# Two halves of the probabilities' lower parts on POOL, and transposes 30 matmuls behind their tile

## The chip, the cores and the metric

The kernel runs on one core of a Trainium2 chip. The metric is the device time of one execution in microseconds. Engines are named as in the profile: PE (TensorE, with PEld for its weight loads), DVE (VectorE), ACT (ScalarE), POOL (GpSimd), SP (SyncE, which issues the DMAs here).

## What is computed

A two-layer diffusion backbone over 1024 latent tokens and 256 context tokens with 1024 channels. Layer 0 mixes tokens with a convolution module, layer 1 with grouped-query attention (16 query heads, 4 key heads, head width 64); each layer ends in a squared-ReLU MLP with 4096 hidden channels. The part that matters here, from the reference:

```python
def gqa_project(h, w_qkv, q_norm, k_norm):
    qkv = h @ w_qkv
    q = qkv[..., :nq]...   # 16 heads of 64
    k = qkv[..., nq:nq + nk]...   # 4 heads of 64
    v = qkv[..., nq + nk:]...
    return rms_norm(q, q_norm), rms_norm(k, k_norm), v

ql = apply_axial_rope(ql, tables)
kl = apply_axial_rope(kl, tables)
...
s = jnp.einsum('bkgqd,bkld->bkgql', q, k).astype(jnp.float32) * (q.shape[-1] ** -0.5)
p = jax.nn.softmax(s, axis=-1).astype(v.dtype)
return jnp.einsum('bkgql,bkld->bkgqd', p, v)
...
def sq_relu_mlp(h, w1, w2):
    return jnp.square(jax.nn.relu(h @ w1)) @ w2
```

## The kernel before

Every matmul of a product works on float32 data split in two parts: a high part (rounded to float32r, made by ACT or DVE) and a lower part (the difference, made by POOL or DVE). A product is three matmuls, high by high, low by high and high by low (`mm3`, L213 to 219).

*Weights.* `unit` (L191 to 211) loads 128x1024 of weights into a `raw` buffer, ACT makes the high part, POOL the lower part in two instructions of 512 columns (or DVE in one of 1024). Both parts lie in a tile `wsp` of the ring `w8` with 5 buffers. While `self.six` names spare tiles, every sixth unit goes to these instead, and is then called `wx`.

*Layer 0's MLP and the projection.* The MLP runs over three token blocks of 416 to 432 columns, each in 8 chunks `c` of 4 hidden tiles: matmuls `ps<-h` (w1), then `ps<-hb` (w2). In the last block, `hook` interleaves layer 1's projection at the ends of chunks. The tokens are taken as A (0 to 384, three tiles of 128), D (384 to 512 and 1024 to 1280, three tiles) and C (512 to 1024, four tiles). `qkv_mm` (L924 to 956) makes for group g = 0 (keys and values), 1 and 2 (queries, 8 heads each) the product of each tile in a PSUM tile `pa`; after a tile's last matmul `qkv_post` (L958 to 989) follows:

- `head_norm`: ACT squares, DVE sums by head (`vh`, L872), takes the reciprocal root in small steps (`rs_s`, `rs_y`, L233 to 236) and multiplies (`kn`, L876).
- `head_parts`: `kn` times the cosines into `o` (POOL, L892), `kn` with halves swapped times the sines (`t`, DVE, L896), their sum (L898); then ACT makes the high part of `qs` or `ks` (L899) and DVE the lower (L900).
- `transpose_out` (L903 to 912): for each four heads four PE transposes into a PSUM tile `tp`, ACT's copy into the single buffer `sb`, and SP's store to `qt` or `kt` in DRAM.

A and D pass `late` empty, C passes it set. The code calls `transpose_out` directly behind `head_parts`. A scheduler orders each engine's instructions by dependencies and priorities, so that some matmuls of the next tile can stand between a tile's last matmul and its transposes. The engines run what they have strictly in their order.

*Attention.* Eight groups `n` (two blocks of 512 queries, four key heads), each with 40 steps `u`, one for each of 4 query heads and 10 key tiles. A step's `stage1` (L1074 to 1089): two matmuls make the scores `sT` (L1077, L1078), ACT the exponentials `e` (L1080), then the high part `p[:, 0]` (DVE's cast at L1083 in odd steps, ACT at L1085 in even ones) and the lower part `p[:, 1]` at L1087: by DVE in every fourth step, in every second at a group's ends and in the last group, else by POOL. `stage2`, five steps later, is three matmuls into `O` (L1093 to 1095). Beside the steps, PE makes the scores of the next group once more for their row maxima (L1040), which DVE reduces out of two PSUM banks (`m`, L1042), and at the end of a group DVE and POOL make the output's parts (`of`, `at`, `atl`).

Last comes layer 1's MLP (after 2186 us), which the change does not touch.

Of the kernel before, what the change touches and what calls it, by code (L numbers as in the profile page):

```python
# [103 lines left out]


LAG = 5
PT = ['rawm', 'sc', 'qs', 'raw', 'raw', 'raw']
MX0, MXS = 4, 38
HM, HS = 2, [1]
LM, LN, L0, L1 = 4, 2, 2, 38  # L110
WL = [0, 1, 2, 3, 4, 5, 6, 7]
PRE = [15, 30]
BUFS = {"w8": 5, "raw": 3, "rawm": 1, "xu": 3, "hl": 2, "hb": 1, "tmp": 5, "acc": 3, "sc": 1, "qs": 1, "ks": 1,
# [14 lines left out]
class Kern:  # L128
# [84 lines left out]
    def mm3(self, ps, pairs, first=True, last=True):  # L213

        n = len(pairs)
        for i, ((wh, wl), (ah, al)) in enumerate(pairs):
            for t in range(3):
                self.nc.tensor.matmul(ps, lhsT=(wh, wl, wh)[t], rhs=(ah, ah, al)[t], start=first and i == t == 0,  # L218
                                      stop=last and i == n - 1 and t == 2)

    def kpairs(self, w, a, N):
        return [((w[0](k), w[1](k)), (a[0](k)[:, :N], a[1](k)[:, :N])) for k in range(KT)]
# [404 lines left out]
    def layer0(self):  # L627
# [42 lines left out]
        def hook(b, c):  # L670
            if b < 2 and c == HCC[0]:
                self.drain(conv[b + 1])
                self.pw2(b + 1)
                n2[b] = self.norm2_block(b + 1, pl=N2P[b], dve_lo=ND[N2D[b]])
                self.bg.insert(0, n2[b])
            if b == 0 and c == 7:
                self.six = (("qs",), ("rawm",))
                self.bg.append(self.modq)
            if b == 2 and c == 1:
                self.drain(self.modq)  # L680
                self.six = (("sc",), ("rawm",))
            if b < 2 and c == 7:
                self.drain(n2[b])
            if b == 2 and c == 0:
                nc.sync.dma_start(out=self.X2[:, :, 0:80], in_=self.xs[1][:, :, 96:176])
            if b == 2 and c == HCC[1]:
                self.need((1, "cctx", 0))
                self.qkv_setup()
                n2["A"] = self.qkv_norm("A", [(0, 384)], pl=AP[0], dve_lo=ND[AD[0]])
                self.bg.insert(0, n2["A"])  # L690
            if b == 2 and c == HCC[2]:
                self.drain(n2["A"])
                self.run(self.qkv_mm(["A"], (0, 1, 2)))
                n2["D"] = self.qkv_norm("D", [(384, 512), (1024, 1280)], pl=AP[1], dve_lo=ND[AD[1]])
                self.bg.insert(0, n2["D"])
            if b == 2 and c == HCC[3]:
                self.nmx = 12
            if b == 2 and c == HCC[4]:
                self.drain(n2["D"])
                self.dq = self.qkv_mm(["D"], (1,))  # L700
                self.mx = self.first_maxima()
                next(self.mx)
# [39 lines left out]
            next(self.mx)  # L742
        next(self.mx)
        self.run(nC)
        self.first_operands()
        for i, _ in enumerate(self.qkv_mm(["C1", "C2"], (0, 1, 2), True)):
            for _ in range(MXC[i] if i < len(MXC) else 0):
# [4 lines left out]
    def first_maxima(self):  # L752

        nc = self.nc
        t = self.mxt = self.t("xu", [P, KT * 512], "mx", F32R)
        K = self.KA[0] = t[:, 0:TOK]
        Q = self.QA[0] = t[:, TOK:TOK + GRP * 512].rearrange("p (h t) -> p h t", h=GRP)
        m3 = self.t("m3", [P, 4, GRP, 3], "m3")

        for keys, qs, sc in (([(0, 384)], (0, 384), [((0, 1, 2), 0, 384, 0)]),  # L760
                             ([(384, 512), (1024, 1280)], (384, 512), [((3,), 0, 384, 0), ((0, 1, 2, 3), 384, 384, 1)]),
                             ([(512, 1024)], None, [((0, 1, 2, 3), 768, 512, 2)])):
            a = sc[-1][1]
            for k, e in keys:
                nc.sync.dma_start(out=K[:, a:a + e - k].bitcast(F32), in_=self.kt[0, :, k:e])
                a += e - k
            if qs:
                src = self.qt[0:GRP, 0:HD, qs[0]:qs[1]].rearrange("h p t -> p h t")
                nc.sync.dma_start(out=Q[0:HD, :, qs[0]:qs[1]].bitcast(F32), in_=src)
                nc.sync.dma_start(out=Q[HD:P, :, qs[0]:qs[1]].bitcast(F32), in_=src)  # L770
            else:
                nc.sync.dma_start(out=self.V0[:, 6:10, 64:192].bitcast(F32), in_=self.vs[:, 4:8, 0])
                nc.scalar.activation(self.KB[0][0:HD, 768:TOK], K[0:HD, 768:TOK].bitcast(F32), AF.Copy)
            yield
            for qts, k, n, c in sc:
                for qt in qts:
                    for j in range(GRP):
                        s = self.psx("s")
                        nc.tensor.matmul(s[:, :n], lhsT=Q[:, j, qt * P:(qt + 1) * P], rhs=K[:, k:k + n],
                                         start=True, stop=True)  # L780
                        nc.vector.reduce_max(m3[:, qt, j, c:c + 1], s[:, :n], axis=AX.X)
                        yield
        self.M = self.t("ks", [P, 4, GRP, 32], "M")
        nc.gpsimd.memset(self.M, 0.0)
        self.max_row(m3, self.QB[0])
# [93 lines left out]
    def head_parts(self, kn, nh, gain, rope, dst, late, o=None, t2=None):  # L879

        nc = self.nc
        W = nh * HD
        h3 = lambda t: t[:, :W].rearrange("p (h d) -> p h d", h=nh)
        if o is None:
            o = self.t("tmp", [P, 512], "o")
        if rope is None:
            nc.vector.tensor_tensor(h3(o), h3(kn), gain.unsqueeze(1).broadcast_to([P, nh, HD]), ALU.mult)
        else:
            C, S = rope
            if t2 is None:  # L890
                t2 = self.t("acc" if late else "tmp", [P, 512], "t2")
            nc.gpsimd.tensor_tensor(h3(o), h3(kn), C.unsqueeze(1).broadcast_to([P, nh, HD]), ALU.mult)  # L892
            v5 = lambda t: t[:, :W].rearrange("p (h r a d) -> p h r a d", h=nh, r=2, a=2)
            S4 = S.rearrange("p (r a d) -> p r a d", r=2, a=2)
            for a in range(2):
                nc.vector.tensor_tensor(v5(t2)[:, :, :, a], v5(kn)[:, :, :, 1 - a],  # L896
                                        S4[:, :, a].unsqueeze(1).broadcast_to([P, nh, 2, 16]), ALU.mult)
            (nc.gpsimd if "a" in late else nc.vector).tensor_tensor(o[:, :W], o[:, :W], t2[:, :W], ALU.add)  # L898
        nc.scalar.activation(dst[:, :, 0:HD].bitcast(F32R), h3(o), AF.Copy)  # L899
        (nc.gpsimd if "l" in late else nc.vector).tensor_tensor(dst[:, :, HD:P].bitcast(F32R), h3(o), dst[:, :, 0:HD],  # L900
                                                                ALU.subtract)
# [56 lines left out]
    def qkv_post(self, ps, g, t, late, defer=False):  # L958
# [2 lines left out]
        late = LT[g] if late else ""  # L961
        kn = self.head_norm(ps, 8 if g else KVH, late, "acc" if defer else "tmp")
        if g == 0:
            ks = self.qtile("ks")
            self.head_parts(kn, KVH, self.gk, (self.Ck[:, gt], self.Sk[:, gt]) if t < SEQ else None, ks, late)
            vt = self.qtile("vt")
            vps = ps[:, 256:512].rearrange("p (h d) -> p h d", h=KVH)
            nc.scalar.activation(vt[:, :, 0:HD].bitcast(F32R), vps, AF.Copy)
            nc.vector.tensor_tensor(vt[:, :, HD:P].bitcast(F32R), vps, vt[:, :, 0:HD], ALU.subtract)
            nc.sync.dma_start(out=self.vs[:, gt], in_=vt)  # L970
            self.transpose_out(ks, KVH, self.kt, 0, t)
            return

        def rest():
            o = t2 = None
            if defer:
                w = self.t("w8", [P, 2048], "qd")
                qs, o, t2 = w[:, 0:1024].rearrange("p (h d) -> p h d", h=8), w[:, 1024:1536], w[:, 1536:2048]
            elif self.nq % 2 or not late:
                qs = self.qtile("qs")  # L980
            else:
                qs = self.t("rawm", [P, 8, P], "qs")
            self.head_parts(kn, 8, None, (self.Cq[:, gt], self.Sq[:, gt]), qs, late, o, t2)
            self.transpose_out(qs, 8, self.qt, (g - 1) * 8, t)
        self.nq += 1
        if defer:
            self.deferred.append(rest)
# [4 lines left out]
    def attention(self):  # L992
# [81 lines left out]
        def stage1(g, j, kt, n, u):  # L1074
# [9 lines left out]
            else:  # L1084
                nc.scalar.activation(p[:, 0], e, AF.Copy)  # L1085
            lm = LM if n < 7 and L0 <= u % 40 < L1 else LN
            (nc.vector if u % lm == lm - 1 else nc.gpsimd).tensor_tensor(p[:, 1], e, p[:, 0].bitcast(F32),  # L1087
                                                                         ALU.subtract)
            return p

        def stage2(g, kt, p, O):
# [450 lines left out]
    def build(self):  # L1542
# [41 lines left out]
        self.modq = None  # L1584
        self.np = self.nx = self.nu = self.nq = 0
        self.deferred = []
        self.six, self.wide, self.ahead = (("sc",), ("qs",)), False, AHEAD[0]
        self.KA, self.KB, self.QA, self.QB = {}, {}, {}, {}
        self.layer0()
# [62 lines left out]
```

## Time and profile before

| | |
|---|---|
| median of 3 runs | 2880.22 us (2876.2 to 2884.11) |
| profiled execution | 2881.31 us |
| its span | 2879.5 us, mean granted clock 0.987 |
| PE, PEld busy | 95%, 80% of the span |
| DVE, ACT, POOL busy | 70%, 51%, 56% |
| projection of A, from its first matmul to the last transposes | 1241 to 1331 us |
| attention | 1622 to 2186 us |

The span runs from the first to the last instruction of one execution. A row of a waits view reads "engine, tile and line <- what ended the wait: total us, times, longest us". A row of a timeline reads "start, duration, engine, line, operation, out<-in, shape, count [idle time before it <- what ended it]"; rows of one line that follow each other are one row with a count. A row by line reads "line, engine, operation, out<-in, shapes, count | busy us, mean ns | idle us before". The views of one line show duration in ns as min/median/max, then the first and last start.

### The profile page before, as it was taken

How to read it: one execution, taken by the hardware profiler on the slowest of the kernel's cores; microseconds unless marked ns; L12 is line 12 of the kernel's file. 1: busy time of each engine (PE TensorE's matmuls, PEld its weight loads, DVE VectorE, ACT ScalarE, POOL GpSimd, SP SyncE). 2: the span in 40 equal slices, each digit the busy share in tenths (PEclk: the TensorE clock that was granted, in tenths of full speed). 3: DMA queues.
4: the chain of work that ended last, by engine and by line, in shares of the span. 5: the costliest groups of instructions: out<-in, count | busy, mean ns of one | idle time of the engine just before them, and what ended most of it. 6: DMA issues, size and time to landing. Idle time of an engine off the chain costs nothing. (4 is left out here: it accounts for less than half of the span.)

```text
span 2879.5 us, 36460 instructions
## 1 busy us (share of the span) xinstructions
PE 2737.8 (95%) x12634; PEld 2310.6 (80%) x12634; DVE 2022.5 (70%) x3312; ACT 1474.9 (51%) x2370; POOL 1602.5 (56%) x1246
## 2 busy tenths in 40 slices
PE   7999999999988999989998899999999899999999
PEld 2778999999878999978886677776667677888887
DVE  3898988987576131455358899976986565568797
ACT  4553554546444354536345577655676544454332
POOL 3777667677555765455334566654666543434332
PEclk9999999999999999999999999999999999999999
DMA  7554333343887334434444411132105555374452
GB/s 242 169 186 160 130 121 113 111 142 121 288 274 234 125 114 165 132 125 138 129 149 142 133 23 23 23 87 75 23 8 194 176 201 185 133 255 161 161 179 103
DMA packets 176729, 406.70 MB, mean 141 GB/s; under 512 B 21344, under 2 KB 64992, under 8 KB 174496
## 3 DMA queue, kind: packets, MB, share of 16 engines
q1 hardware_dynamic: 176544, 404.37, 43.1%
q8 instruction: 99, 1.62, 0.2%
q14 instruction: 86, 0.70, 0.1%
HBM read 343.49 MB, written 60.82 MB: 140 GB/s over the span
## 5 line engine op out<-in xcount | busy, mean ns | idle before, releaser
L210 POOL TENSOR_TENSOR wsp<-raw,wsp 128x512 fp32r<-128x512 f32 x514 | 669.9, 1331 | 384.6 <-ACT wsp L207 342.9
L218 PE MATMUL ps<-h,wsp 128*128 128x432 f32 (+1 forms) x2832 | 570.5, 359 | 6.4 <-ACT h L318 2.6
L218 PEld LDWEIGHTS ps<-h,wsp 128*128 128x128 f32 x2832 | 532.5, 189 | 41.7 <-issue 7.8
L207 ACT ACTIVATE wsp<-raw 128x1024 fp32r<-128x1024 f32 x291 | 306.4, 1057 | 322.0 <-PE ps L218 181.5
L560 DVE SCALAR_TENSOR_TENSOR cv<-u,taps,cv 128x464 f32<-128x464 f32 (+2 forms) x696 | 422.9, 670 | 3.7 <-ACT cv L557 2.1
L218 PE MATMUL ps<-hb,wsp 128*128 128x432 f32 (+1 forms) x1920 | 396.9, 361 | 15.0 <-DVE hb L443 9.4
L1087 POOL TENSOR_TENSOR p<-e,p 128x512 fp32r<-128x512 f32 x223 | 307.6, 1392 | 163.9 <-ACT p L1085 96.6
L218 PEld LDWEIGHTS ps<-hb,wsp 128*128 128x128 f32 x1920 | 363.8, 190 | 33.2 <-DVE hb L443 12.4
L1192 PE MATMUL b<-u 128*128 128x512 f32 x1344 | 304.8, 389 | 0.0
L1192 PEld LDWEIGHTS b<-u 128*128 128x128 f32 x1344 | 252.3, 188 | 52.4
L1080 ACT ACTIVATE e<-sT 128x512 f32<-128x512 f32 x320 | 185.8, 595 | 124.3 <-PE sT L1078 98.5
L1042 DVE TENSOR_REDUCE m<-s 128x1 f32<-128x512 f32 (+1 forms) x336 | 192.1, 590 | 11.9 <-PE s L1040 10.8
L1202 POOL TENSOR_TENSOR u<-tf,u 128x512 fp32r<-128x512 f32 x56 | 102.8, 1856 | 169.9 <-ACT u L1449 156.9
L465 DVE SCALAR_TENSOR_TENSOR X<-ps,m,X 128x432 f32<-128x432 f32 (+2 forms) x144 | 81.4, 587 | 132.4 <-PE ps L218 132.3
L443 DVE TENSOR_TENSOR hb<-ps,hb 128x432 fp32r<-128x432 f32 (+1 forms) x96 | 57.5, 599 | 137.7 <-ACT ps L442 137.5
L1202 POOL TENSOR_TENSOR wsp<-work,wsp 128x512 fp32r<-128x512 f32 x64 | 91.8, 1456 | 104.8 <-ACT wsp L1354 96.4
L1083 DVE CAST p<-e 128x512 fp32r<-128x512 f32 x160 | 114.5, 717 | 30.2 <-ACT e L1080 26.0
L210 POOL TENSOR_TENSOR wx<-raw,wx 128x512 fp32r<-128x512 f32 x92 | 117.9, 1303 | 29.4 <-ACT wx L207 27.9
L1192 PE MATMUL b<-T,wsp 128*128 128x512 f32 x576 | 133.4, 389 | 0.0
L1094 PE MATMUL O<-p,half 128*128 128x512 f32 x320 | 127.1, 397 | 0.0
L1192 PEld LDWEIGHTS b<-T,wsp 128*128 128x128 f32 x576 | 108.1, 188 | 22.7
L218 PE MATMUL ps<-h,wx 128*128 128x432 f32 (+1 forms) x624 | 125.6, 356 | 0.0
(314 smaller groups left out, 5275.8 us busy)
## 6 DMA issues: line engine op xcount, KB each, us to landing
raw<-in_w SPq DMA_DIRECT2D x232, 512.0 KB, 3.4
raw<-in_pw SPq DMA_DIRECT2D x72, 512.0 KB, 3.3
tf<-hd SPq DMA_DIRECT2D x56, 512.0 KB, 4.2
rawh<-in_wmod SPq DMA_DIRECT2D x79, 256.0 KB, 4.4
raw<-in_qkv SPq DMA_DIRECT2D x36, 512.0 KB, 3.4
rawp<-in_wmod SPq DMA_DIRECT2D x32, 512.0 KB, 4.5
raw<-in_w2s SPq DMA_DIRECT2D x16, 1024.0 KB, 6.8
sc<-in_wmod SPq DMA_DIRECT2D x49, 256.0 KB, 4.5
```

Source lines behind the costliest of these rows:

```text
L207: nc.scalar.activation(hi(c, n), raw[:, c * P:(c + n) * P], AF.Copy)
L210: (eng or nc.gpsimd).tensor_tensor(lo(c, n), raw[:, c * P:(c + n) * P], hi(c, n).bitcast(F32), ALU.subtract)
L218: self.nc.tensor.matmul(ps, lhsT=(wh, wl, wh)[t], rhs=(ah, ah, al)[t], start=first and i == t == 0, stop=last and i == n - 1 and t == 2)
L465: nc.vector.scalar_tensor_tensor(X[:, m, a:a + n], pss[z][:, a:a + n], gates[cc][:, m:m + 1], X[:, m, a:a + n], ALU.mult, ALU.add)
L560: nc.vector.scalar_tensor_tensor(dst, src, tap, acc[z][:, :N], ALU.mult, ALU.add)
L1042: nc.vector.reduce_max(m3[:, qt, j, c:c + 1], s[:, :w], axis=AX.X)
L1080: nc.scalar.activation(e, s, AF.Exp, scale=0.125)
L1083: nc.vector.tensor_copy(p[:, 0], e)
L1087: (nc.vector if u % lm == lm - 1 else nc.gpsimd).tensor_tensor(p[:, 1], e, p[:, 0].bitcast(F32), ALU.subtract)
L1094: nc.tensor.matmul(O[1], lhsT=self.half, rhs=p[:, 0], start=a, stop=False)
L1192: self.nc.tensor.matmul(ps, lhsT=w[t % 2](k), rhs=(ah, ah, al)[t], start=first and k == t == 0, stop=k == 3 and t == 2, skip_group_check=True)
L1202: eng.tensor_tensor(w[:, 1, i:i + n], src[:, i:i + n], w[:, 0, i:i + n].bitcast(F32), ALU.subtract)
```

## The change

Three things change.

1. In `stage1`, POOL makes the lower part of p in two instructions of 256 columns each (`PH = 256`). DVE's share stays one instruction of 512.
2. For A and D, `transpose_out` is not called behind `head_parts` but put in a queue: it is due when 30 more matmuls have been written (`TLAG[0]`), and at least 24 behind the one queued ahead of it (`TLAG[1]`). `mm3` counts the matmuls and calls what is due. So that finished tiles can wait, they alternate between the tags `qs` and `sc` (`slot`); these were spare tiles of `self.six`, which is therefore off from chunk 3 of the last block on. Before the loads that read `kt` and `qt` back, and before C, the queue is emptied.
3. For A and D the product with the cosines, `o`, is made by DVE instead of POOL.

```diff
+TLAG = [30, 24]
...
+PH = 256
...
@@ mm3
+        self.nmm += 3 * n
+        while self.tq and self.tq[0][0] <= self.nmm:
+            self.tq.pop(0)[2]()
+
+    def later(self, tag, g, f):
+        self.tdue = max(self.nmm + TLAG[0], self.tdue + TLAG[1])
+        self.tq.append((self.tdue, tag, f, g))
+
+    def slot(self):
+        tag = ("qs", "sc")[self.nslot % 2]
+        self.nslot += 1
+        while any(x[1] == tag for x in self.tq):
+            self.tq.pop(0)[2]()
+        return tag
...
@@ hook, end of chunk 3 of the last block
                 self.drain(n2["A"])
+                self.six = None
                 self.run(self.qkv_mm(["A"], (0, 1, 2)))
...
@@ head_parts
-            nc.gpsimd.tensor_tensor(h3(o), h3(kn), C.unsqueeze(1).broadcast_to([P, nh, HD]), ALU.mult)
+            (nc.gpsimd if late else nc.vector).tensor_tensor(h3(o), h3(kn), C.unsqueeze(1).broadcast_to([P, nh, HD]), ALU.mult)
...
@@ qkv_post, queries
-            self.transpose_out(qs, 8, self.qt, (g - 1) * 8, t)
+            out = lambda: self.transpose_out(qs, 8, self.qt, (g - 1) * 8, t)
+            if late:
+                out()
+            else:
+                self.later(tag, g, out)
...
@@ stage1
-            (nc.vector if u % lm == lm - 1 else nc.gpsimd).tensor_tensor(p[:, 1], e, p[:, 0].bitcast(F32),
-                                                                         ALU.subtract)
+            if u % lm == lm - 1:
+                nc.vector.tensor_tensor(p[:, 1], e, p[:, 0].bitcast(F32), ALU.subtract)
+            else:
+                for i in range(0, 512, PH):
+                    nc.gpsimd.tensor_tensor(p[:, 1, i:i + PH], e[:, i:i + PH], p[:, 0, i:i + PH].bitcast(F32),
+                                            ALU.subtract)
```

What it moves, at three places. First PE's row in the projection of A, from behind its 68th matmul (before) and from its first (after); `pa<-wsp` and `pa<-wx` are matmuls of the product, `tp<-ident` the transposes. Before:

```order
L909 MATMUL tp<-ident,ks 128x128 x4
L218 MATMUL pa<-wx,hq 128x512 x4
L218 MATMUL pa<-wsp,hq 128x512 x12
L909 MATMUL tp<-ident,ks 128x128 x4
L218 MATMUL pa<-wsp,hq 128x512 x15
L909 MATMUL tp<-ident,ks 128x128 x4
L218 MATMUL pa<-wsp,hq 128x512 x50
L909 MATMUL tp<-ident,qs 128x128 x8
L218 MATMUL pa<-wsp,hq 128x512 x13
L218 MATMUL pa<-wx,hq 128x512 x4
L909 MATMUL tp<-ident,qs 128x128 x8
```

After:

```order
L221 MATMUL pa<-wsp,hq 128x512 x72
L933 MATMUL tp<-ident,ks 128x128 x4
L221 MATMUL pa<-wsp,hq 128x512 x30
L933 MATMUL tp<-ident,ks 128x128 x4
L221 MATMUL pa<-wsp,hq 128x512 x24
L933 MATMUL tp<-ident,ks 128x128 x4
L221 MATMUL pa<-wsp,hq 128x512 x24
L933 MATMUL tp<-ident,qs 128x128 x8
L221 MATMUL pa<-wsp,hq 128x512 x24
L933 MATMUL tp<-ident,qs 128x128 x8
```

The transposes of a tile stand 24 to 30 matmuls apart and behind more of the next tiles' matmuls, and no matmul reads a `wx` tile.

Second, DVE's row at a query tile of A, from `kn` to the lower part of `qs`. Before:

```order
L876 TENSOR_TENSOR kn<-pa,rs_y 128x512
L896 TENSOR_TENSOR t_11105<-kn,aux 128x16x16 x2
L872 TENSOR_REDUCE vh<-sq 128x8
L898 TENSOR_TENSOR o<-o,t_11105 128x512
L873 TENSOR_SCALAR vh<-vh 128x8
L900 TENSOR_TENSOR qs<-o,qs 128x8x64
```

After:

```order
L900 TENSOR_TENSOR kn<-pa,rs_y 128x512
L916 TENSOR_TENSOR o<-kn,aux 128x512
L920 TENSOR_TENSOR t_11096<-kn,aux 128x16x16 x2
L896 TENSOR_REDUCE vh<-sq 128x8
L922 TENSOR_TENSOR o<-o,t_11096 128x512
L897 TENSOR_SCALAR vh<-vh 128x8
L924 TENSOR_TENSOR qs<-o,qs 128x8x64
```

DVE has one more instruction for each tile, `o`; POOL's row has one less.

Third, POOL's row from the start of the attention on. Before:

```order
L892 TENSOR_TENSOR qd<-kn,aux 128x512 x2
L1087 TENSOR_TENSOR p<-e,p 128x512 x40
L1133 TENSOR_TENSOR atl_14910<-of,at 128x512
L1087 TENSOR_TENSOR p<-e,p 128x512
L1133 TENSOR_TENSOR atl_14910<-of,at 128x512
L1087 TENSOR_TENSOR p<-e,p 128x512 x28
```

After:

```order
L916 TENSOR_TENSOR qd<-kn,aux 128x512 x2
L1127 TENSOR_TENSOR p<-e,p 128x256 x80
L1173 TENSOR_TENSOR atl_14934<-of,at 128x512
L1127 TENSOR_TENSOR p<-e,p 128x256 x2
L1173 TENSOR_TENSOR atl_14934<-of,at 128x512
L1127 TENSOR_TENSOR p<-e,p 128x256 x56
```

Each instruction on p has become two of half the width; their order among the others is the same. PE, ACT and SP have the same rows in the attention as before, and every engine has the same rows in the MLP of layer 1.

More of the change, by code (lines that the diff above doesn't have):

```diff
@@ L744, in layer0 @@
         self.run(nC)
+        while self.tq:
+            self.tq.pop(0)[2]()
         self.first_operands()
@@ L763, in first_maxima @@
             a = sc[-1][1]
+            while any(x[3] < 2 for x in self.tq):
+                self.tq.pop(0)[2]()
             for k, e in keys:
@@ L963, in qkv_post @@
         if g == 0:
-            ks = self.qtile("ks")
+            tag = "ks" if late else self.slot()
+            ks = self.t(tag, [P, 4 if late else 8, P], "ks")[:, 0:4]
             self.head_parts(kn, KVH, self.gk, (self.Ck[:, gt], self.Sk[:, gt]) if t < SEQ else None, ks, late)
@@ L970, in qkv_post @@
             nc.sync.dma_start(out=self.vs[:, gt], in_=vt)
-            self.transpose_out(ks, KVH, self.kt, 0, t)
+            out = lambda: self.transpose_out(ks, KVH, self.kt, 0, t)
+            if late:
+                out()
+            else:
+                self.later(tag, g, out)
             return
@@ L978, in rest @@
                 qs, o, t2 = w[:, 0:1024].rearrange("p (h d) -> p h d", h=8), w[:, 1024:1536], w[:, 1536:2048]
-            elif self.nq % 2 or not late:
+            elif not late:
+                tag = self.slot()
+                qs = self.t(tag, [P, 8, P], "qs")
+            elif self.nq % 2:
                 qs = self.qtile("qs")
@@ L983, in rest @@
             self.head_parts(kn, 8, None, (self.Cq[:, gt], self.Sq[:, gt]), qs, late, o, t2)
-            self.transpose_out(qs, 8, self.qt, (g - 1) * 8, t)
+            out = lambda: self.transpose_out(qs, 8, self.qt, (g - 1) * 8, t)
+            if late:
+                out()
+            else:
+                self.later(tag, g, out)
         self.nq += 1
@@ L1086, in stage1 @@
             lm = LM if n < 7 and L0 <= u % 40 < L1 else LN
-            (nc.vector if u % lm == lm - 1 else nc.gpsimd).tensor_tensor(p[:, 1], e, p[:, 0].bitcast(F32),
-                                                                         ALU.subtract)
+            if u % lm == lm - 1:
+                nc.vector.tensor_tensor(p[:, 1], e, p[:, 0].bitcast(F32), ALU.subtract)
+            else:
+                for i in range(0, 512, PH):
+                    nc.gpsimd.tensor_tensor(p[:, 1, i:i + PH], e[:, i:i + PH], p[:, 0, i:i + PH].bitcast(F32),
+                                            ALU.subtract)
             return p
@@ L1586, in build @@
         self.deferred = []
+        self.tq, self.tdue, self.nmm, self.nslot = [], 0, 0, 0
         self.six, self.wide, self.ahead = (("sc",), ("qs",)), False, AHEAD[0]
```

## Prediction

> **What bounds the kernel now.** I read the page first, then the busy time by stretch, then who made TensorE wait in the two stretches that the change touches, then single instructions in order of time.
>
> ```profile
> PE 2737.8 (95%) x12634; PEld 2310.6 (80%) x12634; DVE 2022.5 (70%) x3312; ACT 1474.9 (51%) x2370; POOL 1602.5 (56%) x1246
> ```
>
> TensorE is busy 95% of the span, so a change gains only where it waits, and the working of this change reaches two stretches: the query, key and value projection that stands in layer 0's last MLP block (1240 to 1515 us) and the attention (1622 to 2186 us). The busy time by stretch (PE, weight loads, DVE, ACT, POOL, each with its count; then the granted clock):
>
> ```profile
> 1240.00:1345.00 105.00, 90.38 (x436) 75.84 (x435) 68.91 (x137) 52.31 (x100) 52.50 (x41) 0.98 0.46 141
> 1340.00:1400.00 60.00, 60.00 (x307) 57.27 (x307) 20.36 (x26) 32.47 (x55) 30.72 (x27) 1.00 0.41 129
> 1622.00:2186.00 564.00, 533.08 (x2212) 394.14 (x2212) 484.67 (x737) 378.90 (x649) 343.56 (x249) 0.99 0.17 42
> 1690.00:1756.00 66.00, 63.28 (x266) 46.77 (x265) 59.82 (x96) 46.72 (x81) 44.27 (x33) 1.00 0.15 30
> ```
>
> In the first stretch TensorE stands idle 14.6 us; the plain MLP beside it (second row) has no gap at all. In the attention it idles only 31 us by this view, and DVE is busy 91% of one group of heads (fourth row). But busy hides stalls: matmuls overlap, and undisturbed ones start 0.23 us apart:
>
> ```profile
> 1803.15 0.39 PE L1077 MATMUL sT<-mx,H 128*128 128x512 f32 x1
> 1803.38 0.40 PE L1078 MATMUL sT<-QB,H 128*128 128x512 f32 x1
> ```
>
> At 0.23 us the 2212 matmuls of the attention are 509 us (less, since some are narrower), so at least 55 of its 564 us are lost. Who made TensorE wait: the projection first (1240 to 1345), then the attention, matmuls and weight loads:
>
> ```profile
> PE tp L909 <- DVE qs L900: 5.2, 3, 2.6
> PE tp L909 <- DVE ks L900: 4.2, 3, 2.8
> PE tp L909 <- DVE rs_y L233: 3.5, 2, 2.4
> PE tp L909 <- ACT sb L911: 1.7, 1, 1.7
> ...
> PE s L1040 <- DVE m L1042: 14.6, 32, 1.0
> PE sT L1077 <- ACT e L1080: 5.0, 14, 1.3
> ...
> PEld s L1040 <- DVE m L1042: 47.9, 92, 1.4
> PEld O L1095 <- POOL p L1087: 1.1, 3, 0.5
> ```
>
> In the projection all 14.6 us are transposes (tp) that stand right behind their tile while DVE still makes it. In the attention the matmuls of the maxima (L1040) wait for a PSUM bank that DVE's in-order queue has not yet read; POOL's lower parts are almost never what ends a wait.
>
> **Why DVE is late there.** DVE and POOL hold each other up. Two places, in order of time:
>
> ```profile
> 1711.96 1.74 POOL L1133 TENSOR_TENSOR atl<-of,at 128x512 fp32r<-128x512 f32 x1
> 1713.67 1.46 POOL L1087 TENSOR_TENSOR p<-e,p 128x512 fp32r<-128x512 f32 x1
> 1713.07 0.92 DVE L1083 CAST p<-e 128x512 fp32r<-128x512 f32 x1
> 1714.51 1.17 DVE L1087 TENSOR_TENSOR p<-e,p 128x512 fp32r<-128x512 f32 x1
> ...
> 1415.38 2.54 POOL L210 TENSOR_TENSOR wsp<-raw,wsp 128x512 fp32r<-128x512 f32 x2
> 1415.48 1.21 DVE L235 SCALAR_TENSOR_TENSOR rs_s<-rs_s,rs_y 128x8 f32<-128x8 f32 x1
> 1416.72 1.22 DVE L236 SCALAR_TENSOR_TENSOR rs_y<-rs_s,rs_y 128x8 f32<-128x8 f32 x1
> ```
>
> The cast ends 0.29 us behind POOL's instruction (1713.99 against 1713.70), the subtraction 0.55 us behind the next one (1715.68 against 1715.13): each waited for POOL's running instruction to end and then did its own work. And POOL's next one, ready at 1713.67, took 1.46 us: DVE went first. The second place is a picture of two halves: DVE's tiny L235 waits out the first, is let in, and L236 waits out the second.
>
> **The change, part by part.** *Halves of p.* The prices:
>
> ```profile
> L1087 POOL TENSOR_TENSOR p<-e,p x223: 1265/1296/2271, 1627.3 to 2180.4; 128x512 fp32r<-128x512 f32 x112
> L320 POOL TENSOR_TENSOR hC<-t,hC x8: 736/742/743, 1505.8 to 1539.7; 128x256 fp32r<-128x256 f32 x8
> L1083 DVE CAST p<-e x160: 355/580/1526, 1628.1 to 2182.2; 128x512 fp32r<-128x512 f32 x160
> L1083 DVE CAST p<-e 128x512 fp32r<-128x512 f32 x160 | 114.5, 717 | 30.2 <-ACT e L1080 26.0 <-POOL wsp L210 3.7
> L1087 DVE TENSOR_TENSOR p<-e,p x97: 671/1167/1781, 1629.1 to 2182.7; 128x512 fp32r<-128x512 f32 x97
> L1087 DVE TENSOR_TENSOR p<-e,p 128x512 fp32r<-128x512 f32 x97 | 107.4, 1108 | 1.4
> ```
>
> A 256-column subtraction on POOL takes 0.742 us against 1.296 for 512, so two cost 1.484: 0.188 more for each of 223, 42 us of POOL. That lies in POOL's idle time (44.3 of 66 us busy; 31 of them in that group make 5.8 us more). The Trainium skill (GPSIMD Engine Reference, Reconciling with measured numbers) gives 4497 ns for 2048 columns. As an estimate from that page and the slope of the two rows here (2.16 ns a column), the fixed part would be some 65 ns and the cost 15 us of POOL; no row here is that wide, and the two rows decide.
>
> The gain is DVE's. Against their shortest, the 160 casts lose at most 160 x (0.717 - 0.355) = 58 us and the 97 subtractions 97 x (1.108 - 0.671) = 42 us: 100 us, nearly all in waiting for POOL. What is left of a POOL instruction when DVE arrives shrinks with its length (742/1296 = 0.57), and POOL is busy 1.14 times as long (1484/1296): 0.65 of 100 stays, 35 us of DVE's 485 go. The ends: 43 us without the second factor; nothing where two such DVE instructions follow each other, as at 1416, and pay a half each.
>
> What TensorE has of it: its losses to DVE lie between 14.6 us (matmul row) and 47.9 (weight loads); nearer the upper one, since 55 are lost in all, I take 37. These waits are about 0.5 us each (47.9/92), and a queue with two or three DVE instructions that lose 0.36 to 0.44 us each, a third less after the change, is 0.3 to 0.4 us earlier. Half of 37 goes: 19 us (ends 0 and 37). Back go 2 us: each p is done later by 0.19 us or more, and the waits for ACT's e (5.0 us), whose buffers p's last reader frees, grow by a third. **Net 17 us.**
>
> *Transposes 30 matmuls later.* Around the first query tile:
>
> ```profile
> 1275.82 7.33 PE L218 MATMUL pa<-wsp,hq 128*128 128x512 f32 x31
> 1285.51 1.06 PE L909 MATMUL tp<-ident,qs 128*128 128x128 f32 x8 [2.37 <-DVE rs_y L233]
> 1277.11 0.69 DVE L872 TENSOR_REDUCE vh<-sq 128x8 f32<-128x512 f32 x1 [5.92 <-ACT sq L871]
> 1290.24 0.69 DVE L898 TENSOR_TENSOR o<-o,t 128x512 f32<-128x512 f32 x1 [0.59 <-POOL o L892]
> 1284.68 0.68 DVE L900 TENSOR_TENSOR qs<-o,qs 128x512 fp32r<-128x512 f32 x1
> 1291.70 0.69 DVE L900 TENSOR_TENSOR qs<-o,qs 128x512 fp32r<-128x512 f32 x1 [0.70 <-ACT qs L899]
> ```
>
> From the reduction to the finished tile DVE needs 8.25 us (1277.11 to 1285.36), with ScalarE's square ahead of it about 9. The new place is 30 x 0.23 = 6.9 us behind the tile, with another tile's transposes between 7.5 us: the first of a run still waits 1.5 to 2 us. The next ones follow 24 matmuls plus eight transposes apart, 24 x 0.23 + 0.9 = 6.4 us; DVE now takes 7.0 (1284.68 to 1291.70), of which POOL's o costs 0.59 and then moves to DVE at 0.69, the price of L898. So DVE keeps pace only to about half a microsecond a tile. I leave 0.6 us for the three key tiles, 3 for the first group of queries, 1 for the second (its transposes stand among MLP matmuls, farther back) and 1 for sb: 5.6 of 14.6 remain, 9 go, and with them about 1 us of lowered clock (0.98 over 105 us is worth 2). **10 us**, ends 3 and 15.
>
> With the transposes move ScalarE's copy into sb and SP's store to kt and qt. The store now stands behind weight loads on SP; what reads it back comes with the first maxima, after 1420 us. The copy waits on ScalarE for the moved transposes, and weight copies are queued behind it. Should it wait there 1 us, the ring of weight units, below, hides it; uncovered it is the same 1 us for the next unit. No term of its own.
>
> The single D tiles gain less, since matmuls already stood between:
>
> ```profile
> 1424.03 1.33 PE L909 MATMUL tp<-ident,qs 128*128 128x128 f32 x8 [4.45 <-DVE qs L900]
> 1416.47 3.10 PE L218 MATMUL ps<-hb,wsp 128*128 128x432 f32 x15
> PE rb L269 <- DVE dg L265: 4.3, 1, 4.3
> ```
>
> Fifteen matmuls become twenty: 5 x 0.2 = **1 us** of the 4.45. The broadcast rb waits 4.3 us for dg behind the tile's chain on DVE; dg now stands ahead of the sum that it followed (0.7 us), but rb stands 3 matmuls earlier (0.7) and o is on DVE (0.7), against shorter waits for POOL. **1 us** gained, ends -1 and 3.
>
> *The weight ring.* With the wx tiles gone from here, every unit takes one of five w8 buffers. A unit's copy and lower part need some 1.1 us of ScalarE and 2.6 of POOL; a w1 unit feeds 24 matmuls, 4.7 us, and the MLP stretch has no idle TensorE and POOL half idle. Nothing, covered by that half; uncovered, 2.6 us for each group, three in all: end 8.
>
> Sum: 17 + 10 + 1 + 1 = 29. The profiled execution took 2881.3 us (span 2879.5), 1.1 above the median: 2852 against it, **2851** as a median.
>
> **Rivals.** (1) *POOL becomes the attention's bound, and the kernel is slower.* In the group from 1690, 31 p and 3.4 us of other work fill 66 us once a p takes 2.02 us: 1.484 plus 0.27 of waiting for DVE before each half. Should each half wait 0.33, the group lasts 70 us; seven such groups add 28, less 12 from the projection: 2897. For it: each DVE instruction let in costs POOL 0.29 to 0.55. Against: today's mean p is only 0.1 above its median. Chance 0.08.
> (2) *DVE is not let in between the halves*, so that the change doesn't do what it says: the waits stay, 1.14 times as many, 14 us of DVE and some 5 of TensorE; with 12 gained, 2874. Against it stands the row at 1415, with two halves of a weight unit. Beside it, the Trainium skill (GPSIMD Engine Reference, Instruction dispatch) says that a GpSimd core goes on to the next instruction as soon as its share is done, which would leave the gap closed; the trace disagrees at 1415. Chance 0.12.
> (3) *DVE alone sets the projection*: its queue is as long as before, only 3 us go there, 2859. Chance 0.1.
> (4) *The attention loses nearly all its DVE waits*, 37 and a few that follow them: 2829. Chance 0.12.
>
> **How the numbers follow.** The forecast has 0.58, for itself 2840 to 2861. The range 2829 to 2874 takes in (2), (3) and (4) and leaves out (1) and tails. A measurement tells 0.3%, 8.6 us: the forecast, (3) and (4) are faster (0.80), (2) is the same (0.12), (1) slower (0.08).
>
> **What would show it.** After: mean cast in the attention near 0.58 us and DVE's subtraction near 0.93, POOL's p near 0.8 each; L1040's weight loads waiting under 30 us; the projection's transposes waiting under 6 us between 1240 and 1345; the MLP still without gaps. The prediction is wrong if casts stay at 0.7 us, if waits of O or e for POOL grow past 10 us, or if transposes still wait 10 us.

## The result, and the profile after

The changed kernel takes 2862.48 us (median of 6 runs, 2858.3 to 2870.02) against 2881.97 for the kernel before beside it: ratio 0.9933, 95% interval 0.9914 to 0.9951, 19.5 us less. Forecast were 2851 (2829 to 2874) and 29 us less. Sign and range held, but 9.5 us of the gain are missing, and the median lies 1.5 us outside the 2840 to 2861 that the working gave the forecast itself. The profiled execution took 2866.08 us (span 2864.3), 3.6 above its median.

Two stretches are compared throughout: the attention, from the first score matmul (`sT`) to the end of the last O matmul, and the projection, from the first `pa` matmul to the first score matmul. Here are the first and last starts of the first `pa` and `sT` groups, before:

```profile
L218 PE MATMUL pa<-wsp,hq x294: 387/393/776, 1240.9 to 1514.4; 128*128 128x512 f32 x147
L1077 PE MATMUL sT<-mx x80: 388/395/792, 1623.3 to 1991.0; 128*128 128x512 f32 x80
```

After:

```profile
L221 PE MATMUL pa<-wsp,hq x336: 387/394/794, 1243.3 to 1516.0; 128*128 128x512 f32 x168
L1113 PE MATMUL sT<-mx x80: 388/395/796, 1622.6 to 1981.2; 128*128 128x512 f32 x80
```

The projection went from 382.4 us (1623.3 less 1240.9) to 379.3: 3 of the 12 us forecast for it. The last O matmul ended at 2184.3 before and 2168.5 after, so the attention went from 561.0 to 545.9: 15 of 17.

**The attention** gained nearly what the working said. By line (busy us, mean ns | idle before), after:

```profile
L1127 POOL TENSOR_TENSOR p<-e,p 128x256 fp32r<-128x256 f32 x446 | 367.8, 855 | 90.7 <-ACT p L1121 60.4 <-DVE p L1119 19.8 <-PE sT L1114 6.2
L1119 DVE CAST p<-e 128x512 fp32r<-128x512 f32 x160 | 103.2, 646 | 41.8 <-ACT e L1116 35.8 <-POOL wsp L213 5.1 <-PE O L1135 0.3
L1124 DVE TENSOR_TENSOR p<-e,p 128x512 fp32r<-128x512 f32 x97 | 85.7, 884 | 1.4
```

The cast fell from 717 to 646 ns, DVE's subtraction from 1108 to 884: 160 x 0.071 + 97 x 0.224 = 33 us of DVE, where 35 were forecast. POOL pays for it with 2 x 0.855 = 1.71 us for each p. Who made TensorE and its weight loads wait there (1622 to 2186 us):

```profile
PE s L1076 <- DVE m L1078: 5.6, 16, 1.0
...
PEld s L1076 <- DVE m L1078: 32.4, 89, 1.3
PEld sT L1113 <- ACT e L1116: 19.1, 39, 1.6
PEld O L1135 <- POOL p L1127: 1.5, 4, 0.6
```

The waits for DVE's maxima fell from 14.6 to 5.6 us (matmuls) and from 47.9 to 32.4 (weight loads), and O still waits for POOL next to nothing.

**The projection** lost its old waits and got others. Busy time and granted clock by stretch, after, and then who made TensorE wait from 1240 to 1345 us:

```profile
1240.00:1345.00 105.00, 94.08 (x427) 79.85 (x426) 68.81 (x143) 47.78 (x88) 40.03 (x31) 0.92 0.44 134
1340.00:1400.00 60.00, 60.00 (x306) 57.20 (x305) 20.34 (x32) 34.62 (x61) 32.94 (x28) 1.00 0.39 122
```

```profile
PE tp L933 <- ACT sb L935: 3.0, 1, 3.0
PE tp L933 <- DVE rs_y L252: 2.6, 1, 2.6
PE pa L221 <- DVE vt L994: 2.4, 1, 2.4
PE pa L221 <- DVE kn L900: 1.9, 1, 1.9
PE tp L933 <- DVE qs L924: 1.0, 1, 1.0
```

TensorE is busy 94.08 us there instead of 90.38, yet the granted clock fell from 0.98 to 0.92, and the number of matmuls done did not rise (427 against 436; some records can be missing). The longest wait is new: transposes that wait for ScalarE's copy into `sb`. Behind it the granted clock is 0.59 and 0.56 in two slices of 4 us (1330 to 1338). What held ScalarE, in order of time on ScalarE, SP and TensorE:

```profile
1309.62 0.58 ACT L935 ACTIVATE sb<-tp 128x512 f32<-128x512 f32 x1
...
1316.82 0.60 ACT L935 ACTIVATE sb<-tp 128x512 f32<-128x512 f32 x1 [6.12 <-DMA qt<-sb]
```

```profile
1311.21 0.35 SPq L200 DMA_DIRECT2D raw<-in_w  x1
1311.65 1.34 SPq L936 DMA_DIRECT2D qt<-sb  x1
```

```profile
1330.03 0.66 PE L933 MATMUL tp<-ident,qs 128*128 128x128 f32 x4 [3.01 <-ACT sb L935]
```

The copy of 1309.62 is done at 1310.20. Its store stands behind a weight load that SP issues at 1311.21, once a `raw` buffer is free; the store goes out at 1311.65 and has landed at about 1316.8. So 1.45 us of the wait are the queue (1310.20 to 1311.65) and some 5.2 the way from issue to landing. The next copy needs the one `sb` buffer, so ScalarE, in its order, stands still for 6.12 us with its weight copies and squares behind it. In the whole stretch, before and after (waits, and the stores with their median from issue to landing):

```profile
ACT sb L911 <- DMA qt<-sb: 6.0, 5, 2.0
```

```profile
qt<-sb SPq DMA_DIRECT2D x12, 256.0 KB, 2.5
```

```profile
ACT sb L935 <- DMA qt<-sb: 11.6, 4, 6.1
```

```profile
qt<-sb SPq DMA_DIRECT2D x12, 256.0 KB, 3.3
```

### The profile page after: what moved, and what is told of

The parts are those of the page before. It is cut to its first block, busy times and chain, and to the rows that moved or that the text cites. A ratio compares the mean times of both kernels' runs of the same rounds, so it can differ in the third digit from the quotient of the medians.

```text
span 2864.3 us, 36684 instructions
## 1 busy us (share of the span) xinstructions
PE 2739.5 (96%) x12634; PEld 2318.0 (81%) x12634; DVE 1992.2 (70%) x3324; ACT 1473.4 (51%) x2370; POOL 1644.5 (57%) x1457
## 5 line engine op out<-in xcount | busy, mean ns | idle before, releaser
L213 POOL TENSOR_TENSOR wsp<-raw,wsp 128x512 fp32r<-128x512 f32 x526 | 681.7, 1323 | 449.0 <-ACT wsp L210 421.5
L221 PE MATMUL ps<-h,wsp 128*128 128x432 f32 (+1 forms) x2880 | 584.2, 361 | 7.6 <-POOL h L339 3.4
L221 PEld LDWEIGHTS ps<-h,wsp 128*128 128x128 f32 x2880 | 545.1, 190 | 44.6 <-issue 9.3
L210 ACT ACTIVATE wsp<-raw 128x1024 fp32r<-128x1024 f32 x299 | 315.1, 1057 | 332.6 <-PE ps L221 185.0
L1127 POOL TENSOR_TENSOR p<-e,p 128x256 fp32r<-128x256 f32 x446 | 367.8, 855 | 90.7 <-ACT p L1121 60.4
L221 PE MATMUL ps<-hb,wsp 128*128 128x432 f32 (+1 forms) x1992 | 407.5, 360 | 12.9 <-DVE hb L462 7.7
L221 PEld LDWEIGHTS ps<-hb,wsp 128*128 128x128 f32 x1992 | 375.6, 189 | 31.4 <-DVE hb L462 10.2
L1119 DVE CAST p<-e 128x512 fp32r<-128x512 f32 x160 | 103.2, 646 | 41.8 <-ACT e L1116 35.8
L213 POOL TENSOR_TENSOR wx<-raw,wx 128x512 fp32r<-128x512 f32 x80 | 102.3, 1301 | 26.7 <-ACT wx L210 26.2
L221 PE MATMUL ps<-h,wx 128*128 128x432 f32 (+1 forms) x576 | 115.8, 356 | 0.0
```

Source lines behind the costliest of these rows:

```text
L210: nc.scalar.activation(hi(c, n), raw[:, c * P:(c + n) * P], AF.Copy)
L213: (eng or nc.gpsimd).tensor_tensor(lo(c, n), raw[:, c * P:(c + n) * P], hi(c, n).bitcast(F32), ALU.subtract)
L1119: nc.vector.tensor_copy(p[:, 0], e)
L1127: nc.gpsimd.tensor_tensor(p[:, 1, i:i + PH], e[:, i:i + PH], p[:, 0, i:i + PH].bitcast(F32), ALU.subtract)
```

## The experiments

Each kernel is timed against the kernel before on the same chip. "Projection" and "attention" are read from one profile each, as above; five profiles have the changed kernel's projection as it is (after, after_again, late_only, quarters and no_read) and gave 374.0 to 381.3 for it, so a difference of 5 us there says nothing by itself. The part of the projection that belongs to A stands in brackets: from the first `pa` matmul to the first `ps<-hb` behind it, the same 216 `pa` matmuls, 60 transposes and 96 `ps<-h` matmuls in every kernel. The last four rows were run together.

| kernel | median us | before | ratio, 95% interval | projection (A) | attention |
|---|---|---|---|---|---|
| before | | | | 382.4 (94.5) | 561.0 |
| after | 2862.48 | 2881.97 | 0.9933, 0.9914 to 0.9951 | 379.3 (95.9) | 545.9 |
| after_again (the same kernel) | 2863.87 | 2884.01 | 0.9936, 0.9922 to 0.9951 | 374.0 (91.2) | 545.4 |
| halves_only | 2869.21 | 2884.78 | 0.9944, 0.9930 to 0.9958 | 383.5 (94.7) | 545.5 |
| late_only | 2880.33 | 2884.78 | 0.9986, 0.9973 to 0.9999 | 381.3 (96.1) | 562.1 |
| sb_alt | 2861.26 | 2884.78 | 0.9916, 0.9901 to 0.9930 | 371.6 (87.5) | 547.2 |
| act_store | 2863.34 | 2884.78 | 0.9922, 0.9908 to 0.9937 | 375.9 (90.0) | 546.7 |
| quarters | 2876.88 | 2884.01 | 0.9980, 0.9968 to 0.9992 | 376.6 (92.8) | 561.7 |
| no_read | 2846.52 | 2884.01 | 0.9880, 0.9859 to 0.9901 | 374.0 (91.4) | 531.2 |
| sb_alt_vt | 2857.08 | 2884.01 | 0.9906, 0.9895 to 0.9918 | 372.3 (89.2) | 545.6 |
| sb_alt_again | 2859.00 | 2882.80 | 0.9917, 0.9903 to 0.9931 | 371.9 (87.7) | 543.5 |
| sb_alt_lag48 | 2851.96 | 2882.80 | 0.9892, 0.9874 to 0.9910 | 366.1 (87.0) | 544.8 |
| sb_alt_o_pool | 2870.73 | 2882.80 | 0.9957, 0.9944 to 0.9970 | 385.9 (95.8) | 546.4 |
| vt_lag48 | 2852.67 | 2882.80 | 0.9901, 0.9883 to 0.9918 | 366.9 (86.9) | 545.7 |

**The halves alone** (`halves_only`): the kernel before with only part 1 of the change.

```diff
+PH = 256
...
-            (nc.vector if u % lm == lm - 1 else nc.gpsimd).tensor_tensor(p[:, 1], e, ...)
+            if u % lm == lm - 1:
+                nc.vector.tensor_tensor(p[:, 1], e, ...)
+            else:
+                for i in range(0, 512, PH):
+                    nc.gpsimd.tensor_tensor(p[:, 1, i:i + PH], e[...], ...)
```

> The kernel before with POOL's lower parts of p in two halves, and nothing else changed. The prediction's first term says 17 us faster than before; the changed kernel's trace (its attention is 15 us shorter, its projection only 3) says 15. Attention 547 to 552 us, mean cast 0.65 us, projection as before. Rival: the 19 us of the change come from both parts in like measure; then this kernel gains about 10.

15.6 us less. The attention is that of the changed kernel to 0.4 us, and the projection that of before.

**The late transposes alone** (`late_only`): the changed kernel with `PH = 512`, so that p is whole.

```diff
-PH = 256
+PH = 512
```

> The changed kernel with p in one instruction of 512 columns again, so the late transposes and o on DVE alone. The prediction's terms say 12 us faster than before. The changed kernel's trace says 2 to 4: the first matmul of the projection to the first score of the attention took 379.3 us against 382.4. Rival: no gain or a loss of a few us, since every longer wait left there is followed by a stretch of half clock.

4.5 us less, with an interval that reaches almost to nothing (0.9999). With the 15.6 above that is 20.1, and both together measured 19.5: the parts add up within the noise, and most of what is missing is missing in the projection. ScalarE's wait for the store and the clock are as in the changed kernel:

```profile
ACT sb L935 <- DMA qt<-sb: 11.9, 4, 6.3
```

```profile
1240.00:1345.00 105.00, 93.93 (x427) 79.84 (x426) 65.89 (x136) 43.42 (x77) 37.20 (x28) 0.92 0.43 131
```

**Two buffers for the transposed tiles** (`sb_alt`, and again as `sb_alt_again`): for A and D, ScalarE's copies alternate between `sb` and `ks`, which the change leaves unused there.

```diff
-            sb = self.qtile("sb")
+            self.nsb += 1
+            sb = self.qtile("sb" if late or self.nsb % 2 else "ks")
```

> The changed kernel, but the transposed tiles of A and D go in turn to two buffers (sb, and ks, which is free there) instead of one. Theory S (ScalarE stands in its queue until the one sb buffer's store has landed, and that store stands on SP behind weight loads that wait for a raw buffer): ScalarE's waits for stores between 1240 and 1345 us fall from 11.6 us to under 4, TensorE's from 10.9 us to under 7, and the kernel is 3 to 6 us faster than the changed one. Theory D (DVE's queue alone sets the pace of the projection): within 2 us of the changed kernel.

> The kernel with two buffers for the transposed tiles again, as the base for the three runs beside it. Both theories: the projection (first pa to first score) 371 to 374 us, 0.991 to 0.993 of before, some 4 to 8 us under the changed kernel.

0.9916 and 0.9917 against 0.9933 and 0.9936: some 4 to 5 us more gain, twice alike, though the intervals overlap each time. ScalarE no longer waits for a store, and the projection takes 371.6 and 371.9 us, 10.8 and 10.5 less than before, close to the 12 forecast. A's part takes 87.5 and 87.7, under all five profiles with one buffer (91.2 to 96.1). The stretch, and TensorE's waits in it (of `sb_alt`):

```profile
1240.00:1345.00 105.00, 98.15 (x470) 83.87 (x469) 72.02 (x148) 58.97 (x110) 44.26 (x36) 0.97 0.46 141
```

```profile
PE pa L221 <- DVE vt L995: 2.4, 1, 2.4
PE pa L221 <- DVE kn L900: 1.9, 1, 1.9
PE tp L933 <- DVE rs_y L252: 0.7, 1, 0.7
PE tp L933 <- ACT ks L936: 0.7, 1, 0.7
PE st L272 <- DVE acc L305: 0.7, 1, 0.7
PE tp L933 <- DVE qs L924: 0.5, 1, 0.5
```

470 matmuls in the same 105 us, against 427 (450 in after_again). Transposes now wait 1.9 us (3.6 in the second profile), and most of the rest are waits for PSUM tiles of `pa` that DVE has not read yet: there TensorE has run ahead of DVE.

**The stores on another queue** (`act_store`): one `sb` buffer as in the change, but ScalarE issues the stores of A and D itself, so that they stand behind no weight load.

```diff
-            nc.sync.dma_start(out=dram[base + q:base + q + 4, ...], in_=sb)
+            (nc.sync if late else nc.scalar).dma_start(out=dram[base + q:base + q + 4, ...], in_=sb)
```

> The changed kernel, but ScalarE issues the stores of A's and D's transposed tiles itself, right behind its copy, instead of SP behind the weight loads; one buffer as before. Theory S: ScalarE's waits for these stores fall to about 2 us each (the landing alone), none of 6 us; 2 to 5 us faster than the changed kernel. Theory D: within 2 us of it.

```profile
ACT sb L935 <- DMA qt<-sb: 9.3, 5, 3.6
```

The longest wait falls from 6.1 to 3.6 us, the sum only to 9.3, 1.9 us a wait as theory S had it: most of the sum is the landing, not the queue. Its ratio, 0.9922, lies between the change and the two buffers and can be told from neither.

**Quarters** (`quarters`): the changed kernel with `PH = 128`.

```diff
-PH = 256
+PH = 128
```

> The changed kernel with POOL's lower parts of p in four pieces of 128 columns. Theory L (DVE waits for what is left of POOL's running instruction, and each piece costs POOL a fixed 0.19 us): a piece is about 0.46 us, the mean cast falls from 0.65 us to about 0.55 and DVE's subtraction from 0.88 to about 0.8, but POOL has about 80 us more (410 to 490 of some 550 us) and the attention's matmuls begin to wait for POOL: 0 to 15 us slower than the changed kernel. Rival: the fixed part is paid only once (pieces run on in a stream), POOL stays near 430 us, and the kernel is 4 to 8 us faster than the changed one.

13 us slower than the changed kernel on the same chip. Lines and waits in the attention (1622 to 2172 us):

```profile
L1127 POOL TENSOR_TENSOR p<-e,p 128x128 fp32r<-128x128 f32 x880 | 453.9, 553 | 20.8 <-ACT p L1121 14.7 <-DVE p L1119 5.9
...
L1124 DVE TENSOR_TENSOR p<-e,p 128x512 fp32r<-128x512 f32 x92 | 72.8, 791 | 1.3
```

```profile
PEld sT L1113 <- ACT e L1116: 31.3, 51, 2.3
PEld s L1076 <- DVE m L1078: 25.0, 57, 2.3
PEld O L1135 <- POOL p L1127: 12.6, 14, 2.0
```

DVE gains once more (791 ns; 804 over all 97, to the end of this attention at 2185 us), and the waits for its maxima shrink (25.0). But four pieces are 4 x 0.553 = 2.21 us of POOL for each p, beyond the 2.02 at which the prediction's rival (1) said that POOL fills a group. POOL sits idle 20.8 us instead of 90.7, and what waits now is O for p (12.6 us) and the scores for ScalarE's e (31.3 against 19.1), whose buffers POOL frees late: ScalarE's e waits 35.2 us for POOL's p here, 8.6 in the changed kernel (1622 to 2186 us). The rival's mechanism is real; two pieces of 0.855 lie below its point, four beyond.

**POOL writes without reading** (`no_read`): POOL fills its share of p's lower parts with zeros; those lower parts are left out of the result.

```diff
-                for i in range(0, 512, PH):
-                    nc.gpsimd.tensor_tensor(p[:, 1, i:i + PH], e[...], p[:, 0, ...], ALU.subtract)
+                nc.gpsimd.memset(p[:, 1].bitcast(F32), 0.0)
```

> The changed kernel with POOL's lower parts of p left out: POOL writes zeros there in one instruction, so that it reads nothing. Theory L as a ceiling: with POOL's reading gone, DVE's subtraction falls to 0.68 us and the cast to 0.42 to 0.6, TensorE's waits for the maxima (L1076 for DVE) fall from 32 us of weight loads to under 20, and the attention is 8 to 20 us shorter than the changed kernel's 547. Rival (the maxima wait for DVE's own work, not for POOL): the attention is within 4 us of the changed kernel's.

By line (1622 to 2172 us) and weight loads' waits (1622 to 2150):

```profile
L1126 POOL MEMSET p<- 128x512 f32 x220 | 121.2, 556 | 323.9 <-PE O L1133 226.2 <-PE s L1076 48.0 <-ACT e L1116 16.1
...
L1119 DVE CAST p<-e 128x512 fp32r<-128x512 f32 x159 | 88.7, 558 | 49.8 <-ACT e L1116 45.3 <-POOL wsp L213 3.2 <-issue 0.4
...
L1124 DVE TENSOR_TENSOR p<-e,p 128x512 fp32r<-128x512 f32 x96 | 65.5, 683 | 1.4
```

```profile
PEld s L1076 <- DVE m L1078: 17.1, 50, 1.1
```

DVE's subtraction takes 683 ns, against 671 for its shortest before: with POOL reading nothing it waits for nothing. The Trainium skill (SBUF — State Buffer, Who interferes with whom) states this: a DVE instruction with two SBUF inputs contends with a GpSimd instruction that reads SBUF, not with one that only writes it; the row of 683 ns agrees. The cast, which has one input, still takes 558 ns at the mean. 65 casts beside which POOL ran nothing took 416; 79 beside zero fills alone 541 (the median is 427, and the delayed ones end some 0.28 us behind the fill); 16 beside POOL's longer instructions 1214. 416, and not the 355 of the shortest, is thus what an undisturbed cast takes. The attention is 14 us shorter than in the changed kernel (545.4 to 531.2). That is what POOL's reading and the length of its work (1.71 us for each p against 0.556) still cost together; this run does not tell them apart.

**v's parts ahead of the key's** (`sb_alt_vt`): two buffers, and for key tiles `vt`, which frees the PSUM tile, is made ahead of `head_parts`.

```diff
-            self.head_parts(kn, KVH, self.gk, ...)
             vt = self.qtile("vt")
...
             nc.sync.dma_start(out=self.vs[:, gt], in_=vt)
+            self.head_parts(kn, KVH, self.gk, ...)
```

> The kernel with two buffers for the transposed tiles, and in qkv_post the parts of v are written ahead of the key's turn instead of behind it, so that the PSUM tile is read earlier. Where TensorE waits 2.4 us for DVE's part of v at 1264 us (with half clock behind it) that goes: 2 to 5 us faster than with two buffers alone (0.84% faster than before). Rival: DVE's work is the same and the wait only moves to the transposes behind it: within 2 us of it.

The wait of `pa` for `vt` halves, from 2.4 to 1.2 us. In time it stands 6.8 us under the changed kernel; its ratio can't be told from two buffers alone, and its A (89.2) is no shorter.

**Later still, and without the move of `o`.** Three kernels beside `sb_alt_again`: the first transposes 48 matmuls behind (`sb_alt_lag48`), `o` back on POOL (`sb_alt_o_pool`), and 48 with v first (`vt_lag48`).

```diff
-TLAG = [30, 24]
+TLAG = [48, 24]
```

> As sb_alt with the first transposes of a run 48 matmuls behind their tile instead of 30. Theory W (the transposes that still wait do so because DVE's chain is longer than 30 matmuls): the 3.2 us before D's first query tile and the 0.7 us of the first transposes in A go, with the slower clock behind them: 3 to 5 us faster than sb_alt. Rival V (PE now only runs ahead until the PSUM banks of pa are full, since DVE's queue sets the pace): the wait moves to pa or stays as long, within 2 us of sb_alt.

```diff
-            (nc.gpsimd if late else nc.vector).tensor_tensor(h3(o), h3(kn), C..., ALU.mult)
+            nc.gpsimd.tensor_tensor(h3(o), h3(kn), C..., ALU.mult)
```

> As sb_alt with o (the product with the cosines of A and D) back on POOL. Theory V (DVE's queue sets the projection's pace): DVE has 0.69 us less for each of 18 tiles, the waits of pa for vt and kn (2.4 and 1.9 us) shrink, 2 to 4 us faster than sb_alt. Rival K (DVE and POOL hold each other up: one more POOL instruction for each tile, for which DVE's next one waits, and POOL's queue of lower parts of weights ahead of it): no gain, 0 to 3 us slower, waits of DVE for POOL's o of 0.5 us and more a tile.

> sb_alt with both v's parts ahead of the key tile's chain and the first transposes 48 matmuls behind. If the gains of the two add up (theory W and the row of pa's wait for vt, 2.4 us): 4 to 7 us faster than sb_alt, projection near 366 us. If they only move waits (rival V): within 2 us of sb_alt.

With 48, 7.0 us less than two buffers beside it by the medians, more than theory W expected, though the intervals overlap; the projection is 5.8 shorter, 5.1 of it behind A. The wait before D's first query tile falls from 3.2 to 1.8 us, and the granted clock over 15 us around it (from 5 us ahead of these transposes) is 1.00 in both kernels with 48 and 0.89 in both profiles with 30: 1.7 us more. The changed kernel's first profile had 1.00 there with the same 3.2 us of wait, so this part is not fixed by the wait, and the rest of the gain stays open. The two waits for `pa` stay (2.4 and 1.7), as rival V had it. v first adds nothing to it (2852.67). The best version is the one with 48: 0.9892 (0.9874 to 0.9910) against 0.9933 (0.9914 to 0.9951) for the change.

With `o` on POOL it is 11.7 us slower than two buffers beside it, and the projection, 385.9 with 95.8 for A, is no shorter than before. Rival K had the direction, and too small a size. DVE and POOL from 1250 to 1335 us, two buffers first (`sb_alt_again`), then with `o` on POOL:

```profile
L920 DVE TENSOR_TENSOR t<-kn,aux 128x256 f32<-128x256 f32 x12 | 4.5, 417 | 0.0
L916 DVE TENSOR_TENSOR o<-kn,aux 128x512 f32<-128x512 f32 x6 | 4.5, 746 | 0.2
```

```profile
L920 DVE TENSOR_TENSOR t<-kn,aux 128x256 f32<-128x256 f32 x12 | 11.8, 1020 | 0.1
L916 POOL TENSOR_TENSOR o<-kn,aux 128x512 f32<-128x512 f32 x6 | 10.1, 1687 | 9.8 <-DVE kn L900 9.8
L922 DVE TENSOR_TENSOR o<-o,t 128x512 f32<-128x512 f32 x6 | 6.1, 1019 | 1.5 <-POOL o L916 1.2
```

POOL's `o`, or a weight's lower part ahead of it, runs while DVE makes `t` from the same `kn`, and DVE's two instructions take 1020 ns each instead of 417. So the extra 4.5 us of DVE for `o` save 7.3 us of `t`, and the chain to the finished tile loses a stretch in which the two engines alternate. TensorE waits 12.3 us there (1240 to 1345 us), against 8.6 with `o` on DVE beside it, at a granted clock of 0.93 against 0.98:

```profile
PE tp L933 <- DVE qs L924: 6.3, 3, 3.8
PE pa L221 <- DVE vt L995: 3.0, 1, 3.0
PE st L272 <- DVE acc L305: 3.0, 1, 3.0
```

## Why the prediction was right, and where it missed

- *The sign and the attention's 17 us: right.* The halves alone measured 15.6. DVE lost 33 us of waiting (35 forecast), though more of it in the subtraction (884 ns, forecast 930) and less in the cast (646, forecast 580): the working measured the cast's loss from its shortest, 355 ns, where an undisturbed one takes 412 at the mean (49 casts of before beside which POOL ran nothing). Half of TensorE's loss was to go; of the weight loads' waits a third went (47.9 to 32.4, forecast under 30), of the matmuls' three fifths. That the sum came out so near is in part two errors that cancel.
- *DVE is let in between the halves: right*, against rival (2); casts would have stayed at 0.717.
- *POOL does not become the bound: right*, and the point given for it agrees with the runs: 1.71 us for each p lies below 2.02 and gained, quarters at 2.21 lie beyond and lost.
- *The projection's 10 us: not reached.* The step that failed is "The copy waits on ScalarE for the moved transposes ... Should it wait there 1 us, the ring of weight units, below, hides it ... No term of its own." The wait was 6.1 us at its longest, and 11.6 in sum where it had been 6.0. The store goes out behind weight loads and lands later, at a median 3.3 us from its issue where it had been 2.5 (the two rows on `qt` of the first section); but with the stores on ScalarE's own queue the median is 2.5 again and the waits still sum to 9.3, so what lengthened them is not fully explained. The working named the store and SP's queue, but priced neither the landing nor the single buffer. A sign of it stood among its rows of before, TensorE's 1.7 us for ScalarE's `sb`, which it counted to the transposes that wait for DVE. A's part, for which the 10 us stood, took 94.5 us before; with one buffer it took 91.2 to 96.1 in five profiles, 93.5 at the mean, so 1 us was gained; with two 87.5 and 87.7, so 7.
- *That two buffers come to 10.8 and 10.5 of the 12 us is in part luck.* 7 of it are A's. The rest of the projection, for which 2 were forecast, gained 3.8, and 3 to 5 with one buffer; 1.3 to 2.9 of that lie in C's stretch (from its first `pa` to the first score), for which no term stood.
- *Rival (3) had the number, 3 us in the projection and 2859, but not the mechanism:* a second buffer leaves DVE's queue as it is and shortens A's part all the same.
- *The clock term had the wrong sign.* A gain of 1 us was put down; in the profiled execution the stretch fell from 0.98 to 0.92, 0.06 x 105 = 6 us. The changed kernel's second profile had 0.95: there ScalarE waited 11.2 us for stores, but the transposes behind it only 0.7 instead of 3.0, and A's part was 4.7 us shorter. So what the single buffer costs differs from one execution to the next.
- *The move of `o` was costed as an even trade* (0.59 of waiting against 0.69 of work). It is not: with two buffers, `o` on DVE is worth 11.7 us. The row that shows it stood in the trace of before (1250 to 1335 us), `t` at 1044 ns where the same shape takes 417 with `o` on DVE and two buffers:

```profile
L896 DVE TENSOR_TENSOR t<-kn,aux 128x256 f32<-128x256 f32 x12 | 12.0, 1044 | 0.2
```

  So what the projection gained hangs on the move of `o`, and not on the later transposes alone: with `o` on POOL, later transposes and two buffers show no gain over the halves alone (0.9957 against 0.9944, with intervals that overlap), and A's part takes 95.8 us where it took 94.5 before. Whether the move of `o` without the later transposes would do as well was not tried.
- *D: about right.* The first query tile's wait fell from 4.45 to 3.2 us, for the 1 us forecast. At the broadcast the wait mostly changed its place: `rb` waited 4.3 us and the row sums `st` ahead of it 0.9; now `st` waits 4.8 (4.0 in the second profile) and `rb` nothing.
- *The weight ring at nothing: right.* The plain MLP stretch has 60.00 of 60.00 us busy without the wx tiles.

## What to carry to other kernels

Cutting an instruction on POOL into pieces frees DVE, but pays only as long as the fixed cost of the extra piece still fits into POOL's idle time: work out the length of a step at which POOL fills the stage, and stop splitting before it. When work is moved away from a wait, follow every buffer that it uses to the end of the transfer that frees it: a single buffer whose store takes 3 to 5 us to land becomes the next wait, on an engine that stands in order. And an operation on POOL that overlaps DVE's work on the same tile may cost DVE more than doing it there: compare DVE's mean beside it with its mean where POOL is idle.

## What the runs showed of the hardware

- A short wait can cost more than its own time, in clock. After the 2.44 us in which TensorE waited for `vt`, the same wait in two kernels, 16 matmuls took 5.31 us in the changed kernel (0.33 apart) and 34 took 8.12 with 48 matmuls of delay (0.24 apart); 16 x 0.09 makes 1.4 us. The granted clock stands in the second row of each, 0.59 and 1.00:

```profile
1266.27 5.31 PE L221 MATMUL pa<-wsp,hq 128*128 128x512 f32 x16 [2.44 <-DVE vt L994]
1266.00:1270.00 4.00, 3.73 (x10) 3.04 (x11) 3.59 (x14) 1.42 (x3) 0.00 (x0) 0.59 0.84 260
```

```profile
1261.73 8.12 PE L221 MATMUL pa<-wsp,hq 128*128 128x512 f32 x34 [2.44 <-DVE vt L995]
1260.00:1270.00 10.00, 8.27 (x37) 6.77 (x38) 7.23 (x20) 3.61 (x8) 4.60 (x4) 1.00 0.59 173
```

  The Trainium skill (TensorE: Matmul & The Clock Gate, The HAM clock gate) puts the half clock behind at least one idle window of some 3.4 us; here waits of 2.4 to 2.5 us were followed by a granted clock of 0.50 to 0.58 over the next 2 us in the eight profiles of other kernels that have this wait, and by 1.00 in the one with 48. What decides between the two is open.
- An instruction of POOL that only writes (0.556 us) leaves DVE's subtraction alone (683 ns) and still delays some of its casts (541 ns at the mean beside it, 416 beside nothing).
- POOL's subtraction took 0.46 us at the median for 128 columns, 0.741 for 256 and 1.296 for 512: 0.19 us for each piece and 2.17 ns a column by the wider two, and 128 columns lie on that line (0.46).
